# Memory's keys and values ahead of the first value chunk, and row sums taken from transposed quarters, in a two-layer encoder

## The chip, the cores and the metric

The kernel runs on one core of a Trainium2 chip. Its engines work side by side, each on its own queue in program order: TensorE (PE, with its weight loads shown as PEld), VectorE (DVE), ScalarE (ACT), GpSimd (POOL) and SyncE (SP, which only issues DMAs here). The metric is the device time of one launch in microseconds (us), the median of several runs. Only TensorE's products and transposes write PSUM, the accumulator memory of eight banks; DVE and ACT read it.

## What is computed

A trunk of two layers over 512 tokens of width 1024, with 256 memory tokens. Cut to what matters here:

```python
for i in range(2):
    h = rmsnorm(x, norm_g[i]);  mem_h = rmsnorm(mem, mem_norm_g[i])
    proj = h @ (w_in_a if i == 0 else w_in_b)      # heads, memory queries, gate
    o_mix = mixer_dilated(...) if i == 0 else mixer_axial_gqa(...)
    kv = (mem_h @ w_mem_kv[i])                      # memory's keys and values
    k, v = rmsnorm(kv[keys], kn_g), kv[values]
    o_mem = softmax(rmsnorm(q_mem) @ k.T) @ v
    y = concat(o_mix, o_mem) * silu(gate)
    x = x + y @ w_out[i]
```

All is float32.

## The kernel before

**Products in three passes.** Every float32 operand is split into a rounded part (float32r, "hi") and a remainder ("lo"). `mm3` (line 162) multiplies hi by hi, hi by lo and lo by hi. For a weight piece, 128 x 1024, `W.hi` casts it on ACT (line 285) and `W.lo` takes the remainder on DVE (line 295). For activations `split` (line 155) does the same after a transpose.

**Seven products instead of eight.** The large projections (`s_chunk`, line 352) use a Strassen-like scheme: the activation matrix is cut into four quarters 11, 12, 21, 22 and the weights likewise; seven products need the row sums S1 = 21 - 22, S2 = S1 - 11, S4 = 12 + S2, S3 = 11 - 21 of the activations, and T1 to T4 of the weights. The order of the products is 12, 11, S1, S2, S4, S3, 22. A *group* is the PE work between two calls of `W.advance`: 12 products of 512 columns, or 24 of 256. The sums of the weights are made by DVE (T1, and T2 of the very first chunk) or by DMAs that add into the tile, issued on POOL (T1 of later chunks, T2, T3, T4; lines 247 to 269). The narrower projections (memory's keys and values and half of the output projection) go through `chunk` (line 331) with plain products; one chunk of memory has four groups, each of two weight pieces and 12 products.

**Slots.** PE's groups set the order of everything else. After each group, `Driver.tick` counts one slot and steps the generators that are due: `yield n` means n slots later. `drv.free`, ahead of `W.advance`, steps those that were given to `release`; `drv.spawn` gives one to the tick, behind `W.advance`. `late` and `soon` put an instruction at the end of this tick and at the start of the next. Since each engine's queue keeps program order, what is emitted in a slot stands ahead of all that later slots emit, also if it has to wait.

**The weights.** The class `Weights` walks a plan, `PLAN`, one entry a chunk: `W2` (seven products, 512 wide), `W1` (256 wide), `T2` (a chunk of memory), `O1` (output). Pieces are loaded from DRAM by SP (line 233) while fewer than `KEEP` are live; four rounded pieces are in flight (`RING`), and a piece is cast two groups after it is loaded (`LEAD`). `NM4` = 23 tiles of 128 x 1024 are shared by weights, x, memory, gains and activations; a load waits until one is free.

**The opening.** SP loads one row of gains, then the four x tiles mixed with the first eight weight pieces (lines 839 to 852). PE spreads the gain row over 128 partitions with one-row products (`row_bank`, line 557) and does two further one-row products, `busy(512)`. The first x tile is normalized (`norm_1`: squares on ACT and DVE, the power on POOL; `norm_2`: DVE), its quarter 12 transposed (`put_h`, `turn4`) and the first product starts. The second tile's transposes stand between the first and the second half of the first group (`second`, line 905). `prep` (line 857) makes the rest: tiles 2 and 3, the row sums, their transposes, one kind a slot. `mem_norm(0)` (line 567) loads, normalizes and transposes memory while the first chunk (V of the first attention group, `ev_v0`) runs. Then come `mem_kv(0)`: two chunks of memory, keys (`ev_k`: head norms, transposes) and values (`ev_v`), and the memory queries (`s_chunk(256, H, ev_qm)`), line 959.

**The start of layer 2.** The second half of the output projection (`out_rest`, line 694) runs over four blocks of 128 tokens. For each, `ev_o` (line 1189) stores x1, normalizes it, and after `EO` slots makes the operands of layer 2: blocks 0 and 1 give the quarters 12 and 11 (transposed, split), blocks 2 and 3 give the sums in natural layout on DVE (`sum_h`, `sums_h`), and after block 3 each of S1, S2, S4, S3 and 22 is transposed for both blocks and split (`rest_h`). Meanwhile PE is in `mem_kv(1)` and then in the first projection of layer 2, the memory queries. `setup_b` (line 1221) makes the rotary tables on DVE, one operation a slot, from slot `SET_B` on.

Of the kernel before, what the change touches and what calls it, by code (L numbers as in the profile page):

```python
# [24 lines left out]
XW, BOTH = (1, 2, 0, 5), False  # L25
BULK, ACTIVE, MEM_AT, SET_AT, WARM, MEM_B, PREP_Y, ACC_AT, PREP_B, HALF, SET_B = 2, 2, 5, 15, 1, 12, 1, 4, 1, {"a": 3, "b": 3, "o": 0}, 3
MEM_STEP = 1, 1
MEM_D = 4
PD, W_EARLY = 1, True
EO = 1, 2, 2, 2, 1  # L30
# [5 lines left out]
PLAN = ["W2"] + ["T2"] * 2 + ["W1", "W2s"] + ["W2" if c.isdigit() else "W1" for c in A_ORDER[1:]] + ["W2"] + ["O1"] * 2 + ["T2b"] * 2 + ["W1b"] * 7 + ["W2b"] + ["O1"] * 2  # L36
T1_DMA = 17
KEEP = {"T2": 6, "T2b": 4, "O1": 4, "W1": 9, "W2": 10, "W2s": 9, "W1b": 7, "W2b": 9}
# [86 lines left out]
def trunk_kernel(ctx: ExitStack, tc: tile.TileContext, x, mem, wall, norm_g, mem_norm_g, gcol,  # L125
# [50 lines left out]

    class Weights:
        def __init__(self):
            self.items, self.last, self.need, self.allocs, self.sums = [], [], [], [], []
            self.users = {}  # L180
            d = g = 0
            for c, kind in enumerate(PLAN):
                base = len(self.items)
                if kind in GROUPS:
                    units, nb = GROUPS[kind]
                    for u in range(units):
                        for x in (2 * u, 2 * u + 1):
                            self.items.append((c, "P", x))
                            self.last.append(g + (u + 1) * nb - 1)
                            self.allocs.append(((c, "P", x), d, kind))  # L190
                            self.users[c, "P", x] = 1
                            d += 1
                        self.need += [base + 2 * u + 2] * nb
                    g += units * nb
                else:
                    n = 1 if kind in ("W1", "W1b") else 2
                    at = {k: d + i * n for i, k in enumerate(("21", "11", "12", "22"))}
                    d += 4 * n
# [11 lines left out]
            assert d == wall.shape[0], (d, wall.shape)  # L210
# [65 lines left out]
        def hi(self, force=False):  # L276
            i = self.n_hi
            if i >= len(self.items) or not self.ripe(self.at, self.items[i], force, 1 if self.items[i][1] == "T1" and self.items[i][0] < T1_DMA or self.items[i][:2] == (0, "T2") else None):
# [52 lines left out]
    def chunk(units, nb, group, evac):  # L331

        ps = [None] * nb
        for u in range(units):
# [132 lines left out]
    def turn4(src, hi, lo, mid=None):  # L467

        p = at("xT")
        for k in range(4):  # L470
            T.transpose(p[:, k * 128:(k + 1) * 128], src[:, k * 128:(k + 1) * 128], ident)  # L471
        if mid:
            mid()
        split(hi, lo, p.rearrange("p (k t) -> p k t", k=4))
# [10 lines left out]
    def proj_t(act, sels, evac):  # L485
# [5 lines left out]
        chunk(2, len(sels), group, evac)  # L491
# [32 lines left out]

    def head_sq(p, n=4):
# [31 lines left out]
    def row_bank(name, times=1):  # L557

        r = [at("row") for _ in range(2)]
# [33 lines left out]
    def mem_kv(layer, M):  # L593
# [3 lines left out]
        def ev_k(b, p):  # L597
            r = head_sq(p)
            yield 2
            xn = head_mul(p, r)  # L600
            yield 2
            q = transpose4(xn)
            cs = slice(b * 128, (b + 1) * 128)
            yield from put_norm(q, gk_m[layer], kt_[0][:, :, cs], kt_[1][:, :, cs])

        def ev_v(b, p):

            A.activation(vt_[0][:, b], p, AF.Copy, scale=0.5)
            yield 1
            V.scalar_tensor_tensor(vt_[1][:, b], p, 0.5, vt_[0][:, b].bitcast(F32), ALU.mult, ALU.subtract)  # L610

        proj_t(M, NAT[:2], ev_k)
# [225 lines left out]
    rows = {}  # L838
    nc.scalar.dma_start(ident, ident_d)
    row0 = m4(name="row0")[0:1, :]  # L840
    nc.sync.dma_start(row0, norm_g[0:1, :])
    rows["x0"] = halves(row0)
    for c, n in enumerate(XW):
        nc.sync.dma_start(xt[c], xv[c])
        W.dma(n)
# [3 lines left out]
    nc.sync.dma_start(mask, mask_d)  # L849
    nc.sync.dma_start(tabA, tab_a.rearrange("p (b c d) -> p b c d", b=2, c=4))  # L850
    nc.sync.dma_start(grA[:, 0:3], qn_a[0:1, :, 0:32].to_broadcast([128, 3, 32]))
    nc.sync.dma_start(grA[:, 3:6], kn_a[0:1, :, 0:32].to_broadcast([128, 3, 32]))
    H, H2 = {}, {}
    xb = [halves(t) for t in xt]
    nst = {}

    def prep():

        s1, sums = [], []
        for c in range(2):  # L860
            norm_2(xb[2 + c], nst[2 + c], first)
            s1.append(sum_h(xb[2 + c]))
# [6 lines left out]
    def setup():  # L869

        V.tensor_tensor(gk, gc[:, 0:3], gc[:, 3:6], ALU.mult)
# [10 lines left out]
    first = row_bank("x0", WARM)  # L882

    def busy(n):

        T.matmul(at("busy")[:, 0:n], ones, rows["x0"][0][0:1, 0:n], start=True, stop=True)

    busy(512)
    nst[0] = norm_1(xb[0], True)
    W.hi(True)  # L890
    norm_2(xb[0], nst[0], first, (1,))

    def mid():
        busy(128)
        W.lo()
        nst[1] = norm_1(xb[1], BOTH)

    put_h(H, "12", 0, xb[0][1], mid, True)
    if W_EARLY:
        W.hi(True)  # L900
    norm_2(xb[1], nst[1], first, (1,))
    norm_2(xb[0], nst[0], first, (0,))
    norm_2(xb[1], nst[1], first, (0,))

    def second():

        put_h(H, "12", 1, xb[1][1])
        if not W_EARLY:
            W.hi(True)
        put_h(H, "11", 0, xb[0][0])  # L910
        nst[2] = norm_1(xb[2], BOTH)
        W.lo()
        put_h(H, "11", 1, xb[1][0])
        W.hi(True)
        nst[3] = norm_1(xb[3], BOTH)
# [271 lines left out]
    x1b, sums_b = {}, []  # L1187

    def ev_o(n, b, x1):
        if n:  # L1190
# [5 lines left out]
            x1b[b] = x1  # L1196
# [319 lines left out]
```

## Time and profile before

| | us |
|---|---|
| median of 3 runs | 972.06 (971.13 to 972.48) |
| the profiled execution, whole time | 971.6 |
| its span in the trace | 969.8 |
| PE busy | 949.5 (98%) |
| DVE busy | 793.1 (82%) |
| ACT busy | 675.4 (70%) |

A row of the time-ordered view gives the start, the length, the engine, the line, the operation, the tile written and read, the shape, a count, and in brackets how long the engine stood idle before and what ended that. A row of the chain of waits gives start, length, engine and line. Lines 163 to 165 are the three passes of a product, line 471 the transposes of activations. The trace's spans of PE overlap: one product is shown as 0.39 us long while the next starts 0.23 later. The queue of SP is shown as SPq. Names of tiles: `wl` a loaded weight piece, `wh` and `wo` its parts, `pj` the accumulators of the projections, `xT` and `qT` transposes, `act` the parts of memory (M), `h` and `hS` those of the quarters and the sums.

### The profile page before, as it was taken

The numbers are of one execution on the slowest core, as the hardware profiler recorded it, in microseconds if no ns is written. First come the engines' busy times: TensorE is split into PE (matmuls) and PEld (weight loads), VectorE is DVE, ScalarE is ACT, GpSimd is POOL, SyncE is SP. The second block draws the span as 40 slices with busy tenths as digits, with TensorE's granted clock in tenths as the row PEclk, the third lists the DMA queues.
The fourth block names the chain that finished last, engine by engine and source line by source line (L and its number), as shares of the span: only waits on it lengthen the run. The fifth ranks groups of instructions, "written<-read, shape, count | busy, mean of one in ns | idle before, by whom it ended". The sixth has DMA issues, their size and how long they took to land. (4 is left out here: it accounts for less than half of the span.)

```text
span 969.8 us, 16665 instructions
## 1 busy us (share of the span) xinstructions
PE 949.5 (98%) x5728; PEld 835.8 (86%) x5728; DVE 793.1 (82%) x1413; ACT 675.4 (70%) x1687; POOL 332.7 (34%) x480
## 2 busy tenths in 40 slices
PE   8899999999999999999999999999999999999998
PEld 5689988888888888888899996787999999998776
DVE  6997776888888888888898999769888997779863
ACT  6555689686868686868685667545778887878760
POOL 1122423556454545454736011323233231011011
PEclk9999999999999999999999999999999999999999
DMA  8979846968787868685959889959986696786644
GB/s 331 326 267 336 220 102 170 293 131 259 150 256 154 256 153 261 154 260 131 279 134 233 259 203 272 299 191 351 240 178 148 178 241 166 218 213 163 183 140 130
DMA packets 88982, 209.27 MB, mean 216 GB/s; under 512 B 25281, under 2 KB 36033, under 8 KB 88898
## 3 DMA queue, kind: packets, MB, share of 16 engines
q1 hardware_dynamic: 70034, 146.28, 43.5%
q0 software_dynamic: 17568, 59.78, 32.5%
q10 hardware_dynamic: 1296, 2.16, 0.6%
q8 instruction: 45, 0.74, 0.3%
q14 instruction: 39, 0.32, 0.1%
HBM read 157.79 MB, written 12.65 MB: 176 GB/s over the span
## 5 line engine op out<-in xcount | busy, mean ns | idle before, releaser
L295 DVE TENSOR_TENSOR wo<-wl,wh 128x1024 fp32r<-128x1024 f32 x255 | 314.6, 1237 | 12.3 <-ACT wh L285 11.5
L285 ACT CAST wh<-wl 128x1024 fp32r<-128x1024 f32 x255 | 269.7, 1059 | 75.7 <-PE pj L165 39.8
L163 PE MATMUL pj<-wh,hS 128*128 128x512 f32 (+1 forms) x448 | 164.3, 367 | 0.0
L164 PE MATMUL pj<-wo,hS 128*128 128x512 f32 (+1 forms) x448 | 158.1, 353 | 2.6 <-DVE wo L295 2.6
L165 PE MATMUL pj<-wh,hS 128*128 128x512 f32 (+1 forms) x448 | 158.2, 353 | 0.0
L163 PE MATMUL pj<-wh,h 128*128 128x512 f32 (+1 forms) x336 | 123.4, 367 | 0.0
L164 PE MATMUL pj<-wo,h 128*128 128x512 f32 (+1 forms) x336 | 118.8, 354 | 2.3 <-DVE wo L295 2.3
L165 PE MATMUL pj<-wh,h 128*128 128x512 f32 (+1 forms) x336 | 118.9, 354 | 0.0
L420 POOL TENSOR_TENSOR rstd<-mse,half 128x4 f32<-128x4 f32 (+2 forms) x98 | 100.1, 1021 | 8.2
L164 PEld LDWEIGHTS pj<-wo,hS 128*128 128x128 f32 x448 | 85.0, 190 | 13.4 <-DVE wo L295 3.5
L165 PEld LDWEIGHTS pj<-wh,hS 128*128 128x128 f32 x448 | 84.7, 189 | 12.4 <-DVE hS L160 0.3
L163 PEld LDWEIGHTS pj<-wh,hS 128*128 128x128 f32 x448 | 84.8, 189 | 9.7
L419 POOL TENSOR_SCALAR mse<-hss 128x4 f32<-128x4 f32 (+1 forms) x86 | 44.3, 515 | 129.9 <-ACT junk L529 126.1
L360 ACT COPY sn<-pj 128x512 f32<-128x512 f32 x132 | 73.6, 591 | 14.3 <-PE pj L165 10.7
L529 ACT ACTIVATE junk<-sn 128x128 f32<-128x128 f32 x264 | 79.0, 308 | 0.2 <-DVE sn L371 0.2
L987 POOL TENSOR_TENSOR ta<-sn,tabs 128x128 f32<-128x128 f32 (+1 forms) x64 | 37.2, 584 | 119.7 <-DVE sn L534 91.6
L164 PEld LDWEIGHTS pj<-wo,h 128*128 128x128 f32 x336 | 64.0, 190 | 10.0 <-DVE wo L295 2.8
L165 PEld LDWEIGHTS pj<-wh,h 128*128 128x128 f32 x336 | 63.7, 190 | 9.3 <-DVE h L160 0.2
L163 PEld LDWEIGHTS pj<-wh,h 128*128 128x128 f32 x336 | 63.9, 190 | 7.3 <-ACT h L157 0.2
L377 DVE TENSOR_TENSOR sn<-pj,sn 128x512 f32<-128x512 f32 x99 | 67.5, 683 | 3.0 <-PE pj L165 2.6
L269 POOL DMA_DIRECT2D wl<-wl x33 | 29.3, 886 | 112.4 <-DVE wo L295 70.7
L163 PE MATMUL pj<-hS,wh 128*128 128x256 f32 x192 | 55.9, 291 | 0.0
(229 smaller groups left out, 2457.1 us busy)
## 6 DMA issues: line engine op xcount, KB each, us to landing
wl<-in_wall_dram SPq DMA_DIRECT2D x222, 512.0 KB, 6.9
wl<-wl POOLq DMA_DIRECT2D x64, 512.0 KB, 5.8
wl<-in_wall_dram POOLq DMA_DIRECT2D x42, 512.0 KB, 8.5
acc<-sn POOLq DMA_DIRECT2D x16, 256.0 KB, 5.0
od<-o SPq DMA_DIRECT2D x12, 256.0 KB, 5.2
og<-od SPq DMA_DIRECT2D x12, 256.0 KB, 6.8
odb<-o SPq DMA_DIRECT2D x12, 256.0 KB, 2.7
og<-odb SPq DMA_DIRECT2D x12, 256.0 KB, 3.9
```

What stands on the lines that cost most here:

```text
L163: T.matmul(o, lh, rh, start=start, stop=False, skip_group_check=True)
L164: T.matmul(o, lh, rl, start=False, stop=False, skip_group_check=True)
L165: T.matmul(o, ll, rh, start=False, stop=stop, skip_group_check=True)
L269: G.dma_start(self.tile[key], self.tile[c, "T2", x], accum_op=ALU.add)
L285: A.copy(wh, self.tile[self.items[i]])
L295: V.tensor_tensor(wo, self.tile[key], wh.bitcast(F32), ALU.subtract)
L360: A.copy(t, b)
L377: V.tensor_tensor(t, b, t, ALU.subtract if q == "12" else ALU.add)
L419: G.tensor_scalar(e, ss, EPS, None, ALU.add)
L420: G.tensor_tensor(r, e, half[:, 0:n], ALU.pow)
L529: A.activation(jk, p[:, j * 128:(j + 1) * 128], AF.Square, scale=QS, accum_out=ss[:, j:j + 1])
L987: G.tensor_tensor(ta[:, 0:n], xn[:, 0:n, 0:32], ropeA[:, 0, b, s0:s0 + n], ALU.mult)
```

## The change

**Opening.** Memory's two tiles and its gain row are loaded first, each followed by a weight piece, and x after that. A second gain row, x's, is spread by PE into two more accumulators (`gain`) and copied to SBUF by ACT later; `busy(512)` is dropped. PE begins with the two memory chunks; `ahead`, called before each group of the first one, transposes the second tile's first half ahead of the second group and both second halves ahead of the third. `prep` now does all four x tiles from slot 2 on, one a slot, and the sums from slot 7. The first V chunk follows; `mem_norm(0)` goes. `SEQ` gives the order of the chunks, with the weights in DRAM left where they are. T2 of the first V chunk is a DMA like the others. The loads of mask and rotary tables move into `setup` (slot 15).

**Evacuation of `chunk`.** Accumulators are read from `drv.free`, ahead of the weight work of the next group, instead of from the tick behind it; `ev_k` and `ev_v` are cut accordingly.

**Layer 2.** Each block's quarters are transposed once; the sums are formed from the transposed quarters (one of them in PSUM), already in the layout of the operands, and split without a transpose. Blocks 2 and 3 are done separately, casts on ACT at once, remainders on DVE at the end of the tick. `EO` has six values; `SET_B` goes from 3 to 1.

```diff
-XW, BOTH = (1, 2, 0, 5), False
-PD, W_EARLY = 1, True
-EO = 1, 2, 2, 2, 1
+PD = 2
+EO = 2, 2, 1, 2, 2, 1
+SEQ = [1, 2, 0] + list(range(3, len(PLAN)))
...
-                    if c:
-                        G.dma_start(self.tile[key], self.tile[c, "T1", x], accum_op=ALU.add)
-                    else:
-                        V.tensor_tensor(self.tile[key], self.tile[key], self.tile[c, "T1", x], ALU.add)
+                    G.dma_start(self.tile[key], self.tile[c, "T1", x], accum_op=ALU.add)
...
+                if pre:
+                    pre(u, b)
                 group(w, u, b, ps[b])
                 drv.free()
+                if u == units - 1:
+                    drv.release(evac(b, ps[b]), 2)
                 W.advance()
-                if u == units - 1:
-                    drv.spawn(evac(b, ps[b]), 2)
                 drv.tick()
...
+    def first_t(H, top, c):
+        ps = [(k, turn4(top[j], *slot(H, k, c))) for k, j in (("12", 1), ("11", 0))]
+        for k, p in ps:
+            A.copy(whole(k, c), p)
+    def diffs_t(H, low, c):
+        f22 = whole("22", c)
+        A.copy(f22, turn4(low[1], None, None))
+        p = turn4(low[0], None, None)
+        yield 1
+        s1, s3 = whole("S1", c), whole("S3", c)
+        V.tensor_tensor(s1, p, f22, ALU.subtract)
+        V.tensor_tensor(s3, full["11"][:, :, c * 128:(c + 1) * 128], p, ALU.subtract)
+        split(*slot(H, "S1", c), s1)
+    def rest_t(H, c, ds):
+        def put(k, f):
+            hi, lo = slot(H, k, c)
+            A.copy(hi, f)
+            drv.late(lambda: V.tensor_tensor(lo, f, hi.bitcast(F32), ALU.subtract))
+        cs = slice(c * 128, (c + 1) * 128)
+        s1, s2_, s4, s3, f22 = [full[k][:, :, cs] for k in ("S1", "11", "12", "S3", "22")]
+        V.tensor_tensor(s2_, s1, s2_, ALU.subtract)
+        V.tensor_tensor(s4, s4, s2_, ALU.add)
+        put("S2", s2_)
+        yield ds[0]
+        put("S4", s4)
+        yield ds[1]
+        put("S3", s3)
+        yield ds[2]
+        put("22", f22)
+        yield 1
...
         def ev_k(b, p):
             r = head_sq(p)
-            yield 2
-            xn = head_mul(p, r)
-            yield 2
-            q = transpose4(xn)
+            def rest():
+                xn = head_mul(p, r)
+                yield 2
+                q = transpose4(xn)
...
+            drv.release(rest(), 2)
+            yield 1
...
+    for b in range(2):
+        nc.sync.dma_start(mt[b], mem[b * 128:(b + 1) * 128])
+        W.dma(1)
+    W.dma(2)
...
+    for c in range(4):
+        nc.sync.dma_start(xt[c], xv[c])
+        if c % 2:
+            W.dma(2)
...
     def prep():
+        s1, sums, n = [], [], {}
+        for c in range(5):
+            if c < 4:
+                n[c] = norm_1(xb[c])
+            if c:
+                norm_2(xb[c - 1], n[c - 1], rows["x"])
+                if c > 2:
+                    s1.append(sum_h(xb[c - 1]))
+            if 1 < c < 4:
+                put_h(H, "12", c - 2, xb[c - 2][1])
+                put_h(H, "11", c - 2, xb[c - 2][0])
             yield 1
         for c in range(2):
             sums_h(H, xb[c], xb[2 + c], c, s1[c], sums)
-            yield 1
+            yield 2 - c
         yield from rest_h(H, sums)
...
-    busy(512)
-    nst[0] = norm_1(xb[0], True)
+    mb, M = [halves(t) for t in mt], Act(NM)
+    nst = [norm_1(mb[0], True)]
...
+    def ahead(u, b):
+        if (u, b) == (0, 1):
+            for j in range(2):
+                A.copy(rows["x"][j], gain[j])
+            norm_3(mb[1], M, 128, 0)
+            for c in range(2):
+                norm_2(mb[c], nst[c], first, (1,))
+        if (u, b) == (1, 0):
+            for c in range(2):
+                norm_3(mb[c], M, 128 * c, 1)
...
-    drv.spawn(mem_norm(0), MEM_AT)
-    s_chunk(512, H, ev_v0, pre=second)
-    km, vm = mem_kv(0, Ms[0])
+    km, vm = mem_kv(0, M, ahead)
+    s_chunk(512, H, ev_v0)
...
             if b < 2:
-                put_h(H2, "12", b, x1[1])
-                put_h(H2, "11", b, x1[0])
+                first_t(H2, x1, b)
             else:
-                s1 = sum_h(x1)
+                yield from diffs_t(H2, x1, b - 2)
                 yield EO[2]
-                sums_h(H2, x1b[b - 2], x1, b - 2, s1, sums_b)
-            if b == 3:
-                yield EO[3]
-                yield from rest_h(H2, sums_b, EO[4])
+                yield from rest_t(H2, b - 2, EO[3:])
```

More of the change, by code (lines that the diff above doesn't have):

```diff
@@ L180, in __init__ @@
             self.users = {}
-            d = g = 0
-            for c, kind in enumerate(PLAN):
+            g = 0
+            for c in SEQ:
+                kind, d = PLAN[c], sum(pieces(k) for k in PLAN[:c])
                 base = len(self.items)
@@ L209, in __init__ @@
                             g += 1
-            assert d == wall.shape[0], (d, wall.shape)
+            assert sum(pieces(k) for k in PLAN) == wall.shape[0]
             self.g = -1
@@ L329, in trunk_kernel, with chunk @@
     W = Weights()
-    def chunk(units, nb, group, evac):
+    def chunk(units, nb, group, evac, pre=None):
         ps = [None] * nb
@@ L555, in row_load, with row_bank @@
         rows[name] = halves(t)
-    def row_bank(name, times=1):
-        r = [at("row") for _ in range(2)]
+    def row_bank(name, times=1, bank=at):
+        r = [bank("row") for _ in range(2)]
         for j in (1, 0):
@@ L838, in trunk_kernel @@
     rows = {}
+    mt = [m4(name="m") for _ in range(2)]
     nc.scalar.dma_start(ident, ident_d)
     row0 = m4(name="row0")[0:1, :]
[L841 to L845, printed above, removed]
+    nc.sync.dma_start(row0, mem_norm_g[0:1, :])
+    rows["m0"] = halves(row0)
+    row1 = m4(name="row1")[0:1, :]
+    nc.sync.dma_start(row1, norm_g[0:1, :])
+    rows["x0"] = halves(row1)
+    for b in range(2):
+        nc.sync.dma_start(mt[b], mem[b * 128:(b + 1) * 128])
+        W.dma(1)
+    W.dma(2)
     tabA = s2(name="tabA")[:, 0:256].rearrange("p (b c d) -> p b c d", b=2, c=4)
@@ L880, in setup @@
             yield 1
-    first = row_bank("x0", WARM)
+    first = row_bank("m0", WARM)
+    gain = row_bank("x0", 1, pj)
+    rows["x"] = halves(m4(name="row"))
     def busy(n):
-        T.matmul(at("busy")[:, 0:n], ones, rows["x0"][0][0:1, 0:n], start=True, stop=True)
-    busy(512)
-    nst[0] = norm_1(xb[0], True)
+        T.matmul(at("busy")[:, 0:n], ones, rows["m0"][0][0:1, 0:n], start=True, stop=True)
+    mb, M = [halves(t) for t in mt], Act(NM)
+    nst = [norm_1(mb[0], True)]
     W.hi(True)
-    norm_2(xb[0], nst[0], first, (1,))
+    norm_2(mb[0], nst[0], first, (0,))
     def mid():
@@ L895, in mid @@
         W.lo()
[L896 to L915, printed above, removed]
+        nst.append(norm_1(mb[1]))
+    turn4(mb[0][0], M.block(0, 0, slice(0, 128)), M.block(1, 0, slice(0, 128)), mid)
+    W.hi(True)
+    norm_2(mb[1], nst[1], first, (0,))
+    W.lo()
+    def ahead(u, b):
[8 more added lines that the diff above has]
+                norm_3(mb[c], M, 128 * c, 1)
     drv.spawn(prep(), PD)
```

56 lines of the change are left out of this document (33 added, 23 removed).

## The prediction

> **What bounds the kernel now.** I read the page's busy shares first, then the stretches of 20 us, then TensorE's waits, then the time-ordered rows of the opening and of the start of layer 2.
>
> ```profile
> span 969.8 us, 16665 instructions
> PE 949.5 (98%) x5728; PEld 835.8 (86%) x5728; DVE 793.1 (82%) x1413; ACT 675.4 (70%) x1687; POOL 332.7 (34%) x480
> ```
>
> TensorE (PE) is without work for 20.3 us of 969.8. An edit can help where PE waits, or by taking work from PE itself.
>
> ```profile
> 0.00:20.00 20.00, 16.77 (x51) 10.79 (x52) 11.19 (x18) 12.54 (x26) 4.54 (x16) 1.00 0.90 340
> 20.00:40.00 20.00, 15.42 (x76) 11.83 (x75) 19.97 (x26) 9.58 (x14) 3.69 (x4) 1.00 0.99 296
> ...
> 660.00:680.00 20.00, 18.82 (x109) 15.69 (x108) 19.96 (x29) 10.78 (x29) 7.58 (x8) 1.00 1.04 336
> ```
>
> Columns after the length: PE, weight loads, DVE, ACT, POOL, granted clock, DMA share, GB/s. Both places that the change touches are the ones where PE loses time, and in both DVE is full: 19.97 of 20 us at 20-40, 19.96 at 660-680. The waits name it:
>
> ```profile
> PE pj L164 <- DVE wo L295: 6.7, 8, 2.0
> ```
>
> PE waits there for a weight piece's remainder (line 295), which stands in DVE's queue behind the preparation of activations.
>
> **Prices.** From the time-ordered rows:
>
> ```profile
> 64.20 0.39 PE L163 MATMUL pj<-wh,act 128*128 128x512 f32 x1
> ```
>
> ```profile
> 644.88 0.23 PE pj L165
> 645.10 0.23 PE pj L163
> ...
> 656.88 0.89 PE xT L471 x8
> ```
>
> ```profile
> 46.46 1.29 DVE L160 TENSOR_TENSOR h<-xT,h 128x512 fp32r<-128x512 f32 x2 [1.19 <-ACT h L157]
> 47.67 2.44 DVE L295 TENSOR_TENSOR wo<-wl,wh 128x1024 fp32r<-128x1024 f32 x2
> ...
> 54.41 1.41 DVE L465 SCALAR_TENSOR_TENSOR m<-m,rstd,row 128x512 f32<-128x512 f32 x2
> ```
>
> A 512-column product costs PE 0.228 us (96 of them run from 64.20 to 85.97 below), a transpose 0.11. Two instructions in a row overlap by some 0.08, so DVE pays 0.60 for a 512-wide two-input operation, 1.14 to 1.2 for a 1024-wide one, 0.66 for a normalization.
>
> **The opening, before.**
>
> ```profile
> 0.73 0.35 SPq L841 DMA_DIRECT2D row<-in_norm_g_dram  x1
> ...
> 1.14 0.37 SPq L844 DMA_DIRECT2D x<-in_x_dram  x1
> ...
> 2.24 3.75 PE L562 MATMUL row<-row,ones 1*128 1x512 f32 x4 [2.24 <-DMA row<-in_norm_g_dram]
> ...
> 5.78 1.91 PE L886 MATMUL busy<-row,ones 1*128 1x512 f32 x2
> ...
> 9.65 0.80 PE L163 MATMUL pj<-wh,h 128*128 128x512 f32 x1
> ...
> 10.68 0.63 PE L165 MATMUL pj<-wh,h 128*128 128x512 f32 x1
> ...
> 11.10 0.63 PE L163 MATMUL pj<-wh,h 128*128 128x512 f32 x1
> ...
> 12.38 1.64 PE L471 MATMUL xT<-ident,x 128*128 128x128 f32 x8
> ...
> 14.84 0.66 PE L471 MATMUL xT<-ident,x 128*128 128x128 f32 x4 [0.81 <-DVE h L160]
> ```
>
> ```profile
> 7.06 0.75 DVE L465 SCALAR_TENSOR_TENSOR x<-x,rstd,row 128x512 f32<-128x512 f32 x1 [1.36 <-POOL rstd L420]
> ...
> 7.87 1.11 PE L471 MATMUL xT<-ident,x 128*128 128x128 f32 x4 [0.17 <-DVE x L465]
> ...
> 9.02 0.58 ACT L157 CAST h<-xT 128x512 fp32r<-128x512 f32 x1
> ...
> 85.97 0.60 PE L541 MATMUL qT<-ident,xn 128*128 128x128 f32 x4
> ```
>
> The first product starts at 9.65 and the work of the first V chunk and of memory's keys and values ends at 85.97. It holds 168 + 96 products (60.2 us) and 68 transposes (7.4). So 76.3 - 67.6 = 8.7 us are lost, to waits and to the first products, which run at 0.42 until about 14.
>
> **The opening, after.** Products and transposes are the same in number, so three things decide.
>
> Start. PE gets a second gain row (four passes more at 0.85 each, by the x4 row) and loses the two busy passes: it is free at about 2.24 + 8 x 0.85 = 9.0, not 7.7. The memory tile, one row later in SP's queue (0.4 us), is normalized by 8.2 (x: 7.06 + 0.75), so now PE is late. Four transposes at 0.2, a cast of 0.6 and the hand-over put the first product at 10.7: +1.05.
>
> Slow products. Twelve in a row instead of six broken by transposes; with the same 4 us or so until full pace, 8 to 10 run 0.2 too long: 1.6 to 2.0 us.
>
> DVE. I step the queues in program order, each instruction starting when its engine is free and its inputs are there. From 10.7 to the remainder of V's first piece, DVE has 12 operations of 0.60 (M's 4 remainders, 4 of H, 2 head products, 2 differences), 11 normalizations of 0.66 and 10 of 1.14 (8 weight remainders, 2 T1 sums): 25.9 us. It stands idle 3.2 us for the second half of M and about 2.6 elsewhere, mostly because the first casts of x stand on ACT behind squares and two weight casts. The remainder is done at 42.5. PE by then has 21.9 of products, about 1.8 of slow pace, 36 transposes (3.9) and 2.5 of small waits: 1.2 for M's casts and remainders at the second group, 0.7 at the third, 0.6 for x's differences. That is 40.8. It waits 1.7. The next nine or so microseconds of DVE (three more weight remainders, two S1 remainders, three sums, four halves of memory's keys and values, then the S2 sum of the second block) end at 52.2. The transposes of that S2 block stand in PE's queue at 48.9, because the preparation emits S2 one group after S1, four groups before it is needed: 3.3 more. After that ACT and DVE have air. Waits 7.5, slow pace 1.8, sum 9.3 against 8.7 lost before; with the later start +1.65. The slow products may be ten rather than nine, so I take **+1.9 us**. Bounds: without the 1.7 and the 3.3 it is -3.1; with loads late by 3 us (below) +5.
>
> Hidden, at nothing: the T2 sums of V leave DVE (2 x 1.2) for POOL, whose copies
>
> ```profile
> wl<-wl POOLq DMA_DIRECT2D x64, 512.0 KB, 5.8
> ```
>
> land in about 6 us (median) and are read four groups of 2.7 us after the sum is due; if the cover went, PE would wait once for the difference, under 3. The 512 KB row load goes; two ACT copies replace it in an idle stretch of ACT. Table loads move behind slot 15; they are read by the first head, some 50 us later. SP queues 14 half-megabyte loads at the start instead of 12; at the 340 GB/s of the first 20 us they are in by 21.6 us, x's last tile before that, and it is squared after 30. V's T1 pieces must wait for free buffers (23 in all, 15 held by x, memory, M, its keys, values and row): about 30, read at 33.
>
> **Layer 2.** Ten groups of four transposes (S1, S2, S4, S3, 22 of two blocks) give way to four (22 and 21): 56 transposes become 32, so 24 x 0.11 = **-2.6 us** of PE's own time. DVE has 22 operations before (2 differences, 6 sums, 14 remainders) and 22 after. ACT gets 6 copies more, 0.54 each; it has 9 of 20 us free. The order is what changes:
>
> ```profile
> 657.65 1.42 DVE L465 SCALAR_TENSOR_TENSOR acc<-acc,rstd,row 128x512 f32<-128x512 f32 x2 [1.45 <-DMA x1d<-acc]
> ...
> 663.78 0.22 DVE L1222 TENSOR_SCALAR grB<-grB 128x128 f32<-128x128 f32 x1
> 664.03 0.69 DVE L1225 TENSOR_TENSOR tabs<-tbraw,grB 128x512 f32<-128x512 f32 x1
> ...
> 669.92 0.68 DVE L514 TENSOR_TENSOR xs<-xs,acc 128x512 f32<-128x512 f32 x1
> ...
> 677.00 0.68 DVE L516 TENSOR_TENSOR xs<-acc,xs 128x512 f32<-128x512 f32 x1
> ...
> 688.31 1.20 DVE L295 TENSOR_TENSOR wo<-wl,wh 128x1024 fp32r<-128x1024 f32 x1
> ```
>
> ```profile
> 39.16 1.10 ACT L360 COPY sn<-pj 128x512 f32<-128x512 f32 x2
> ...
> 671.78 1.05 ACT L285 CAST wh<-wl 128x1024 fp32r<-128x1024 f32 x1 [0.81 <-PE pj L165]
> 676.85 1.05 ACT L285 CAST wh<-wl 128x1024 fp32r<-128x1024 f32 x1 [4.02 <-DMA wl<-wl]
> ```
>
> ```profile
> 682.56 0.36 PE L163 MATMUL pj<-wh,hS 128*128 128x256 f32 x1
> ```
>
> DVE runs without a pause from 657.65 to 689.5. Before, the sums went through PE's transposes to ACT; now ACT's casts of S1 and S2 read DVE's sums directly, and DVE is behind. Stepping the queues again: DVE takes up the second block's 12 and 11 remainders at 663.3, after waiting 2 us for ACT, whose copies and head squares stand ahead of those casts. Then come a table (0.6), two normalizations (1.3), two head products (1.2), four weight remainders (4.6), the first quarter differences (1.3) and S1's remainder (0.6): the first S2 sum starts at 674.2 and ends near 675. ACT, in order, does S2's cast then, the second S1 cast after the second difference (676.2), key and value, and only at 677.8 T1's weight cast, 6 us later than the 671.78 above. On DVE T1's remainder stands behind eleven more operations, 8.2 us, and ends at 683.6. PE gets to its first product on S1 (682.56 above) some 2 us sooner by the saved transposes, at 680.6, and that group wants the remainder at once: **+3.0**. The tables, moved two slots up, put 2 to 3 DVE operations into DVE's idle time
>
> ```profile
> 640.00:660.00 20.00, 20.00 (x98) 16.75 (x97) 11.34 (x15) 11.47 (x23) 5.78 (x13) 1.00 0.81 296
> ```
>
> before 660, where it is busy 11.34 of 20 us (a part of that walk; left in place they would make the wait 1.2 longer). Evacuations ahead of weight work cost a remainder 0.6 of delay at most, covered by two groups of lead. 3.0 - 2.6 is 0.4; some of the 1.2 us that PE loses now at 660-680 goes with it, so **+0.2**. Bounds: -2.6 (the remainder is not late) and +2 (it is late again at S2).
>
> Sum: 971.6 (the profiled execution: span 969.8 and 1.8 around it) + 1.9 + 0.2 = 973.7. That execution lies 0.46 under the median of 972.06, so **974.2**.
>
> **Rivals.**
> A, faster: DVE keeps up. If it is idle for less than the 3.2 before M's second half, the S2 transposes find their sum ready and 3.3 goes, with 0.2 of the 1.7; with T1's cast in time layer 2 gives 2.2. 972.06 - 1.6 - 2.2 = 968.3. For: DVE has no more work than before, 2.4 less. Against: both stretches were already full. It decides if DVE is under 3 us behind at V's second group.
> B, they cancel: one of the two late steps comes, the other not; 1.9 - 2.2 or -1.4 + 1.5: 972.
> C, the clock. One-row products kept PE busy from 2.24 to 7.69, yet the pace was 0.42 at 10.7-11.1 (the granted clock reads 1.00 throughout). If eight passes, 6.8 us, release it before the first product, 8 to 12 products and 4 transposes gain 0.2 or 0.1 each, some 2.4: 971.8. [...]
> D, slower by more: T1's piece lands after 33 and its sum, on DVE's in-order queue, holds all preparation behind it. Each microsecond late is one lost; 3.5 gives 977.7. For: DMA's share is 0.90 and 0.99 in the first two stretches, and every buffer is taken. Against: 3 us of margin.
>
> **Numbers.** Forecast 0.35 (973 to 976), A 0.28, B 0.22, C 0.05, D 0.10. This measurement tells about 0.2%, 1.9 us, from no change. Faster is A: 0.28. Same is B, C and the forecast's lower edge (0.05): 0.32. Slower 0.40. The range reaches from A with the T1 wait also gone in full, 967, to D: 978.
>
> **What would show it.** First product at 10.5 to 11. A PE wait for a weight remainder near 41 and for S2's sum near 49, DVE busy over 19 of 20 us at 30-50; the 85.97 work, less its 8 key transposes, ends near 88. In layer 2, 32 activation transposes, and one wait of 2 to 4 us on T1's remainder in the first memory-query groups. I am wrong if 30-50 shows PE at 20 of 20 (then A), or a wait on a weight DMA shows on DVE before 35 (then D).

## The result, and the profile after

The changed kernel takes 976.57 us (median of 6; 975.70 to 978.75), beside 971.60 for the kernel before on the same chip: 1.0053 times as long, 95% interval 1.0041 to 1.0065, some 5 us slower. Of the runs reported below, one execution (of covered_row_loaded) took 1225.66 us at a mean granted clock of 0.717; it is in no ratio. The changed kernel's profiled execution is the slowest of the six, 978.75 us with a span of 976.8, so its end is not compared; its stages are.

In the changed kernel lines 164 to 166 are the three passes of a product, 475 the transposes of activations, 297 the remainder of a weight piece. Its page, span and engines:

```profile
span 976.8 us, 16652 instructions
PE 952.7 (98%) x5706; PEld 837.4 (86%) x5706; DVE 790.2 (81%) x1411; ACT 680.0 (70%) x1695; POOL 342.6 (35%) x482
```

PE is busy 3.2 us longer with 22 instructions fewer. So the loss is not in waits alone: some instructions took longer. The same stretches of 20 us as before (PE, weight loads, DVE, ACT, POOL, granted clock, DMA share, GB/s):

```profile
0.00:20.00 20.00, 16.77 (x40) 9.56 (x41) 7.99 (x13) 10.43 (x19) 2.19 (x10) 1.00 0.89 349
20.00:40.00 20.00, 19.40 (x100) 15.67 (x99) 17.24 (x23) 16.31 (x45) 12.73 (x17) 1.00 0.90 350
40.00:60.00 20.00, 15.34 (x65) 12.14 (x64) 17.15 (x23) 8.20 (x12) 4.42 (x5) 0.83 0.94 221
...
680.00:700.00 20.00, 17.14 (x131) 16.94 (x130) 18.07 (x25) 15.49 (x30) 5.36 (x6) 0.91 1.03 317
```

In the first 20 us PE is busy as long as before (16.77), from 20 to 40 longer (19.40, before 15.42). But 40 to 60, where PE was full before with 106 instructions, has 65, and the granted clock reads 0.83; 680 to 700 reads 0.91. Before, both read 1.00. PE's waits, by what ended them:

```profile
PE pj L165 <- DVE wo L297: 5.1, 4, 2.9
PE xT L475 <- DVE xs L521: 3.2, 1, 3.2
```

Both waits that were forecast are there. In order of time, PE's rows of the opening:

```profile
2.56 7.16 PE L622 MATMUL row<-row,ones 1*128 1x512 f32 x8 [2.56 <-DMA row<-in_mem_norm_g_dram]
...
11.44 0.80 PE L164 MATMUL pj<-wh,act 128*128 128x512 f32 x1
...
44.09 0.50 PE L165 MATMUL pj<-wo,h 128*128 128x512 f32 x1 [1.50 <-DVE wo L297]
...
53.70 1.09 PE L475 MATMUL xT<-ident,xs 128*128 128x128 f32 x4 [3.17 <-DVE xs L521]
54.44 0.78 PE L164 MATMUL pj<-wh,h 128*128 128x512 f32 x1
55.02 0.63 PE L165 MATMUL pj<-wo,h 128*128 128x512 f32 x1
...
59.65 1.03 PE L475 MATMUL xT<-ident,xs 128*128 128x128 f32 x8
60.44 0.48 PE L164 MATMUL pj<-wh,h 128*128 128x512 f32 x1
60.75 0.39 PE L165 MATMUL pj<-wo,h 128*128 128x512 f32 x1
```

Look at the lengths behind the wait of 3.17 us (it begins at 50.53): 0.63 at 55.02, and 0.39 again at 60.75. One product starts every 0.43 us there, half the pace of 0.23, until 59.65. Twelve products take 5.21 instead of 2.74 us, the four transposes 0.74 instead of 0.35: 2.9 us that no wait shows. What the wait was for, DVE's rows of the changed kernel:

```profile
49.35 2.35 DVE L297 TENSOR_TENSOR wo<-wl,wh 128x1024 fp32r<-128x1024 f32 x2
51.62 0.74 DVE L650 SCALAR_TENSOR_TENSOR kmT<-qT,gc,kmT 128x512 fp32r<-128x512 f32 x1
52.28 0.68 DVE L161 TENSOR_TENSOR hS<-xT,hS 128x512 fp32r<-128x512 f32 x1
52.88 0.68 DVE L521 TENSOR_TENSOR xs<-xs,x 128x512 f32<-128x512 f32 x1
```

The S2 sum (line 521) stands behind remainders that nobody needs yet. A mark to compare by are the transposes of `pmt` that wait 0.6 us for ACT near 156 us, past all that the change touches in layer 1. They start at 156.00 before and at 161.43 after: the opening costs 5.4 us in this execution. The mark has a scatter of its own: layer2_alone, whose layer 1 is that of the kernel before, has it at 157.3, since there the first weight piece landed later and the first product started at 10.93 instead of 9.65. In layer 2 the wait for T1's remainder is 2.86 us, and it too is followed by slow products (one in 0.21 instead of 0.12 us), though not at once: the first four run at full pace.

```profile
687.00 0.38 PE L165 MATMUL pj<-wo,hS 128*128 128x256 f32 x1 [2.86 <-DVE wo L297]
687.23 0.28 PE L166 MATMUL pj<-wh,hS 128*128 128x256 f32 x1
...
687.76 0.42 PE L164 MATMUL pj<-wh,hS 128*128 128x256 f32 x1
687.97 0.42 PE L165 MATMUL pj<-wo,hS 128*128 128x256 f32 x1
...
691.11 0.28 PE L165 MATMUL pj<-wo,hS 128*128 128x256 f32 x1
691.23 0.28 PE L166 MATMUL pj<-wh,hS 128*128 128x256 f32 x1
```

From memory's first product of layer 2 to the first product on its keys it is 76.21 us (651.85 to 728.06), beside 76.29 before (647.66 to 723.95): up to there layer 2 costs nothing.

### The profile page after: what moved, and what is told of

Read it like the earlier page. It is cut to its first block, busy times and chain, and to the rows that moved or that the text cites. A ratio compares the mean times of both kernels' runs of the same rounds, so it can differ in the third digit from the quotient of the medians.

```text
span 976.8 us, 16652 instructions
## 1 busy us (share of the span) xinstructions
PE 952.7 (98%) x5706; PEld 837.4 (86%) x5706; DVE 790.2 (81%) x1411; ACT 680.0 (70%) x1695; POOL 342.6 (35%) x482
## 4 chain that ended last, share of the span: by engine, by line
PE 80%; DVE 8%; DMA 7%; ACT 3%; issue 1%; SPq 0%; DVEq 0%; ACTq 0%; POOLq 0%
PE pj L166 21%; PE pj L164 21%; PE pj L165 21%; DMA wl<-in_wall_dram 3%; DVE wo L297 3%; PE qT L601 2%; PE sa L1122 1%; PE oo L1224 1%; PE pt L1203 1%; PE sa L1118 1%; DMA odb<-o 1%; PE ptb L1421 1%; PE ob L165 1%; DMA acc<-sn 1%; ACT wh L287 1%
## 5 line engine op out<-in xcount | busy, mean ns | idle before, releaser
L424 POOL TENSOR_TENSOR rstd<-mse,half 128x4 f32<-128x4 f32 (+2 forms) x98 | 102.9, 1050 | 8.2
```

The source lines that it names most:

```text
L424: G.tensor_tensor(r, e, half[:, 0:n], ALU.pow)
```

## The experiments

"Ratio" is to the kernel before on the same chip, with its 95% interval. "Mark" is the start of those `pmt` transposes in the profile (156.00 before, 161.43 after).

| run | ratio | interval | mark, us |
|---|---|---|---|
| opening_alone | 1.0047 | 1.0030 to 1.0064 | 161.0 |
| layer2_alone | 1.0006 | 0.9993 to 1.0019 | 157.3 |
| s2_two_later | 0.9989 | 0.9978 to 1.0001 | 155.9 |
| fill_products | 1.0022 | 1.0010 to 1.0034 | 158.1 |
| fill_rows | 1.0055 | 1.0034 to 1.0076 | 160.9 |
| both_later | 1.0020 | 1.0008 to 1.0032 | 155.6 |
| s4_sum_later | 1.0012 | 1.0002 to 1.0022 | 155.7 |
| later_prep_sooner | 1.0054 | 1.0036 to 1.0071 | 157.0 |
| later_row_loaded | 1.0013 | 0.9997 to 1.0030 | 154.1 |
| s4_later_row_loaded | 0.9979 | 0.9967 to 0.9991 | 154.5 |
| x3_later | 1.0004 | 0.9991 to 1.0018 | 153.7 |
| covered_row_loaded | 0.9969 | 0.9954 to 0.9983 | 155.9 |

**Which half costs the time.** opening_alone is the changed kernel with `ev_o` and its delays as before; layer2_alone is the kernel before with the new `ev_o`, `first_t`, `diffs_t`, `rest_t`.

> The changed kernel with layer 2 built as before (row sums through ten groups of transposes, its old delays, tables at the third slot). Theory: the opening carries the whole loss. PE waits about 3 us for the S2 sum near 50 us, the products after it run at 0.43 instead of 0.23 us, and the 256-wide memory-query products start 5 to 6 us later than before; 4.5 to 6 us over the kernel before, 976 to 977.6 where that one takes 971.6. Rival: the opening loses only the wait (some 3 us) and the rest is lost in layer 2 and behind it: 974 to 975.

> The kernel before with only layer 2's row sums from transposed quarters (its delays, casts and remainders apart, tables at the first slot). Theory: 24 transposes fewer (2.6 us) and the small waits at 660 to 680 (1.2) against one wait for the remainder of T1 (2.9) and a slow stretch of some 3.5 us after it (1.7): within 1 us of the kernel before, 971 to 972.6. Rival: the loss between 728 and 923 us in the changed kernel comes from layer 2: 2 to 4 us over the kernel before, 973.6 to 975.6.

1.0047 and 1.0006 make up the whole 1.0053. The loss is the opening's; its wait is 3.12 us again. Layer 2 alone can't be told from no change, as the theory had it, but not by the wait that it named. In its profile PE waits for a bank that ACT copies out late, probably because this kernel keeps the old order of evacuations (no run tested that), and no slow stretch follows. That holds for this execution, whose mean granted clock is 1.000; ten of the twelve runs read 0.994 to 0.998.

```profile
682.22 0.39 PE L163 MATMUL pj<-wh,hS 128*128 128x256 f32 x1 [2.61 <-ACT sn L360]
682.45 0.28 PE L164 MATMUL pj<-wo,hS 128*128 128x256 f32 x1
682.56 0.28 PE L165 MATMUL pj<-wh,hS 128*128 128x256 f32 x1
```

**Is it the place of S2's transposes.** In `prep`:

```diff
             sums_h(H, xb[c], xb[2 + c], c, s1[c], sums)
-            yield 2 - c
+            yield 2 + c
```

> The changed kernel with one number changed: layer 1's S2 transposes are emitted two groups later (they are still read two groups after that). Theory: the 3.2 us wait at 50.5 comes only from the place of these transposes in PE's queue; the wait goes, and with it the stretch at half pace behind it (2.4 us): 4 to 5.5 us under the changed kernel, 971 to 972.5, and the granted clock at 40 to 60 us reads 1.00. Rival: DVE is the bound there whatever the order; PE then waits at the next weight remainder instead: less than 1.5 us gained, 975 to 976.5.

0.9989, that is 0.0064 or 6.2 us under the changed kernel's ratio: a little more than expected. The same stretch, of this kernel:

```profile
40.00:60.00 20.00, 18.19 (x89) 14.56 (x88) 19.78 (x26) 10.23 (x14) 4.42 (x5) 1.00 0.98 220
```

Clock 1.00, and of the wait 0.28 us is left, at a weight remainder. DVE now works 19.78 of 20 us, so it has no more to give there, but it needed no more: one number puts the opening level with the one before.

**Is it the wait that slows the products, and what counts as work.** Neither run saves any waiting; both put useless PE work into the wait, ahead of the second block's S2 transposes.

```diff
+    def cover():
+        p = at("busy").rearrange("p (a t) -> p a t", a=2)
+        for _ in range(13):
+            T.matmul(p, part["12"][:, 0, 0, 0:128], part["12"][:, 0, 0:2, :], start=True, stop=True)
...
             for c in range(2):
+                if k == "S2" and c:
+                    cover()
                 put_h(H, k, c, sums[c][i])
```

fill_rows has three `T.matmul(p, ones, rows["m0"][0][0:1, :], ...)` in `cover` instead; the trace shows them as six records.

> The changed kernel with 13 products on old operands (some 3 us of PE, results unused) set into the wait ahead of the second block's S2 transposes. They save no waiting. Theory: the wait itself lets the clock drop, so with PE kept busy the 12 products after it take 0.23 us each, not 0.43, and the granted clock at 40 to 60 us reads 1.00: 2 to 2.5 us under the changed kernel, near 974.3. Rival: the slow pace has another cause than the wait; the products after it stay at 0.43 and the time stays at 976.6 or rises by some tenths.

> The changed kernel with three passes on one row (128 columns out of one partition, 512 wide, some 0.9 us each) set into the wait of 3.2 us instead of 13 products on all rows. If the clock goes by whether PE has instructions, they hold it: products behind the wait at 0.23 us, 2 to 2.5 us under the changed kernel, as with 13 products. If it goes by how much of the array works, one row in 128 is as good as idle: the products behind it run at 0.43 us for 3.4 to 6 us and the time is that of the changed kernel, 1.004 to 1.0065 of the kernel before.

With 13 products in the wait:

```profile
49.76 3.24 PE L505 MATMUL busy<-h 128*128 128x512 f32 x13
53.17 0.63 PE L475 MATMUL xT<-ident,xs 128*128 128x128 f32 x4 [0.16 <-DVE xs L526]
53.55 0.48 PE L164 MATMUL pj<-wh,h 128*128 128x512 f32 x1
53.87 0.40 PE L165 MATMUL pj<-wo,h 128*128 128x512 f32 x1
```

With passes on one row:

```profile
49.88 3.50 PE L505 MATMUL busy<-row,ones 1*128 1x512 f32 x6
53.31 1.11 PE L475 MATMUL xT<-ident,xs 128*128 128x128 f32 x4
54.08 0.78 PE L164 MATMUL pj<-wh,h 128*128 128x512 f32 x1
54.65 0.63 PE L165 MATMUL pj<-wo,h 128*128 128x512 f32 x1
```

The transposes start at about the same time (53.17 and 53.31). Behind the products the pace is 0.23 and the mark comes 3.3 us sooner than after the change (0.3 of it from an earlier start); behind the passes it is 0.43, as behind the idle wait, and the ratio is that of the changed kernel. The granted clock at 40 to 60 us reads 1.00 with the products and 0.83 with the passes, as after the change. So here the idle wait slowed the products, and 3.50 us of passes on one row in its place did not prevent that.

**Layer 2's wait.** Two ways to let T1's remainder pass S2's work. Both are made on s2_two_later. both_later:

```diff
-EO = 2, 2, 1, 2, 2, 1
+EO = 2, 2, 2, 1, 2, 1
```

s4_sum_later keeps `EO` and has in `rest_t`:

```diff
-        V.tensor_tensor(s4, s4, s2_, ALU.add)
         put("S2", s2_)
-        yield ds[0]
+        yield ds[0] - c
+        V.tensor_tensor(s4, s4, s2_, ALU.add)
+        yield 1
         put("S4", s4)
-        yield ds[1]
+        yield 1 + c
```

> The changed kernel with S2 emitted later in both layers: layer 1 as in the run with one number changed; in layer 2 the sums and casts of S2 one group later (third delay 1 to 2), S4 where it was (fourth delay 2 to 1). Theory: T1's weight cast then no longer stands behind the first S2 cast on ACT, and its remainder no longer behind three DVE operations of the second block: it comes some 2.3 us sooner, the wait of 2.9 at the first S1 group shrinks under 1 and, being short, leaves the clock at full speed: 3 to 4 us under the run with layer 1 alone, 0.993 to 0.996 of the kernel before. Rival: DVE works there without a pause, so the wait only moves to S2's remainder one group later: under 1.5 us gained, 0.997 to 0.999.

> The run with layer 1's S2 two groups later, and in layer 2 S2 left where the change put it, but S4's two sums taken out from behind S2's and put behind T1's remainder on DVE; S4's casts of the first block one group later, beside the second's. Theory: DVE, not the order, bounds that place, so only work taken from ahead of T1's remainder counts: two sums of 0.6 make the wait 1.65 instead of 2.85 us, and a wait that short leaves the clock at full pace (1.7 us more); some of it is lost again at S2's group, whose bank DVE frees late: 1.5 to 2.5 us under the run with layer 1 alone, 0.996 to 0.998 of the kernel before. Rival: the wait comes back in full at S2's group, as with S2 later: no gain, 0.999 to 1.002.

Both lose 2 to 3 us to s2_two_later. The first wait shrinks (1.41 and 2.10 us), and a second one comes at S2's group: 3.41 and 2.05. In both_later, PE then DVE:

```profile
679.80 0.38 PE L165 MATMUL pj<-wo,hS 128*128 128x256 f32 x1 [1.41 <-DVE wo L297]
...
686.21 0.35 PE L164 MATMUL pj<-wh,hS 128*128 128x256 f32 x1 [3.41 <-ACT hS L569]
```

```profile
682.78 1.28 DVE L570 TENSOR_TENSOR hS<-f,hS 128x512 fp32r<-128x512 f32 x2
684.77 0.69 DVE L570 TENSOR_TENSOR hS<-f,hS 128x512 fp32r<-128x512 f32 x1 [0.71 <-ACT hS L569]
685.38 0.68 DVE L381 TENSOR_TENSOR sn<-pj,sn 128x512 f32<-128x512 f32 x1
```

The wait is booked on an ACT cast, but S2 accumulates into the bank that line 381 reads, and that read ends at 686.06, just before PE goes on; it stands behind three remainders of activations. That reading is from the rows; no run removed it. The runs fit the rival's mechanism: DVE is short of time there, and the order only chooses who waits. both_later came out worse even than its rival's 0.997 to 0.999, because its two waits add up to 4.82 us where s2_two_later has one of 2.85; either profile has one slow stretch there.

**Gains elsewhere in the opening.** later_prep_sooner is made on both_later:

```diff
-PD = 2
+PD = 1
...
-            yield 2 + c
+            yield 2 + 2 * c
```

x3_later is made on s4_later_row_loaded, in `prep`:

```diff
                 put_h(H, "11", c - 2, xb[c - 2][0])
-            yield 1
+            yield 2 if c == 3 else 1
...
-            yield 2 + c
+            yield 2
```

The loaded row is made on both_later (later_row_loaded) and on s4_sum_later (s4_later_row_loaded):

```diff
-    row1 = m4(name="row1")[0:1, :]
-    nc.sync.dma_start(row1, norm_g[0:1, :])
-    rows["x0"] = halves(row1)
...
         nc.sync.dma_start(xt[c], xv[c])
+        if c == 2:
+            row_load("x", norm_g[0:1, :])
...
-    gain = row_bank("x0", 1, pj)
-    rows["x"] = halves(m4(name="row"))
...
-            for j in range(2):
-                A.copy(rows["x"][j], gain[j])
```

> The kernel with both S2 later, and the preparation of x started one group sooner (its delay 2 to 1; S2 and what follows stay where they were). Theory: DVE is idle for over 5 us at 10 to 30 us and short of time at 35 to 45; moving norms and remainders forward takes the 1.5 us wait for V's first weight remainder near 42.6 away: 1 to 1.5 us under the kernel with both later. Rival: the squares and casts of x then stand on ACT ahead of memory's casts, for which PE waits already (0.7 at 16.6): what is won is lost there, within 0.5 us.

> The kernel with both S2 later, and x's gain row loaded into all partitions by a transfer (512 KB, behind x's third tile) instead of four one-row passes and two copies. Theory: the four passes delay the start; the first product moves from 11.4 to about 10 us, and as passes on one row do not bring the array to full pace anyway, all of it is kept: 1 to 1.5 us under the kernel with both later. Rival: the passes do count for the clock; the products then run at half pace for longer and the two cancel within 0.5 us; or x's last tile and weights come later by the 512 KB and PE waits for them once.

> The kernel with S4's sums later, and x's gain row loaded by a transfer instead of one-row passes. Theory: the first product at 10.0 instead of 11.4 us and all of layer 1 sooner by the same 1.45, as the profile of the same edit showed with both S2 later: 0.9945 to 0.9965 of the kernel before, faster than both kernels. Rival: the later stages take it back (1.9 instead of 0.8 us of waits near 912): within 0.5 us of the run without it.

> The kernel with S4's sums later and the row loaded, and x's last tile normalized and subtracted one group later (S1 of the first block goes one group later too, S2 stays). Theory: two normalizations and a difference (1.9 us of DVE) then stand behind V's weight remainders near 41 instead of ahead, and the 1.5 us wait there goes; some 0.5 comes back near 50, where DVE is busy 19.7 of 20 us: 0.5 to 1.2 us under the run before it. Rival: DVE is the bound over the whole of 35 to 55 us, the wait moves to 50 in full or, over 2.6 us long, costs the clock: no gain or a loss.

Sooner preparation is a miss: 0.0034 slower than both_later. A new wait of 1.10 us at 22.28, for a remainder of memory's activations that x's work now delays on DVE, and the wait near 43 is 1.79 us, no shorter. Its mark is 1.45 us later; besides, the slow stretch of layer 2 is twice as long in its profile (6.8 us, in both_later 3.4). x's last tile later only moves that wait: from 41 to 46, and from 1.53 to 2.40 us. It is a miss too: 0.0025 slower than s4_later_row_loaded, though its profile has the mark 0.7 us sooner; where the runs lose it was not found.

The loaded row moves the first product as forecast, here of later_row_loaded:

```profile
7.53 1.11 PE L475 MATMUL xT<-ident,m 128*128 128x128 f32 x4 [1.50 <-DVE m L469]
8.57 0.79 PE L965 MATMUL busy<-row,ones 1*128 1x128 f32 x2
9.32 0.79 PE L164 MATMUL pj<-wh,act 128*128 128x512 f32 x1
```

9.32 instead of 11.13 us, but then 10 products run slow instead of 8, so the mark moves by 1.45 (1.2 in s4_later_row_loaded). The 10 is not a price of the early start: x3_later starts at 9.24 and has 8 slow ones and part of a ninth (the last section has the other starts). The ratios fall by 0.0007 in the one pair and 0.0033 in the other; the gain that was expected lies between them, but 0.9979 misses the 0.9945 to 0.9965 that were forecast for s4_later_row_loaded, since s4_sum_later, on which it is made, had missed its own 0.996 to 0.998. Both profiles also lose some of the gain near 914 us, where waits of 1.92 and 2.35 us are followed by a slow stretch that the kernels without the loaded row do not have.

**All that helped, with layer 2's wait filled.** covered_row_loaded has s2_two_later's number, the loaded row, `rest_t` as the change has it, and in `s_chunk`, for layer 2's memory queries alone:

```diff
+            if a == cover:
+                p = at("busy").rearrange("p (a t) -> p a t", a=2)
+                for _ in range(10):
+                    T.matmul(p, act["12"][:, 0, 0, 0:128], act["12"][:, 0, 0:2, :], start=True, stop=True)
             if fresh:
...
-    s_chunk(256, H2, ev_qmb)
+    s_chunk(256, H2, ev_qmb, cover="S1")
```

> The kernel with layer 1's S2 two groups later and x's gain row loaded; layer 2 as the change has it, with S4's sums back in their place, and ten products on old operands (2.3 us of PE, results unused) ahead of the first S1 group there. They save no waiting for T1's remainder, they only keep PE at work. Theory: first product at 10.0 us; the wait of 2.85 shrinks to about 0.5, the remainder comes no sooner, and the 14 or more products behind it take 0.12 instead of 0.21 us each: 1.45 and 1.7 us under the run with layer 1's S2 later, 0.995 to 0.9965 of the kernel before, the fastest of all. Rival: the slow stretch comes anyway, from a later wait or because ten products are too few, or the fill delays the transposes and evacuations queued behind it: 0.997 to 0.9985, no better than with S4's sums later.

```profile
679.91 2.46 PE L392 MATMUL busy<-h 128*128 128x512 f32 x10
682.21 0.28 PE L164 MATMUL pj<-wh,hS 128*128 128x256 f32 x1
683.06 0.39 PE L165 MATMUL pj<-wo,hS 128*128 128x256 f32 x1 [0.58 <-DVE wo L297]
...
683.40 0.28 PE L164 MATMUL pj<-wh,hS 128*128 128x256 f32 x1
```

No slow product follows, and at 0.9969 it is faster than both kernels, its interval clear of 1. It falls short of the sum of its parts (0.9989 less 1.45 and 1.7 us, 0.9957): a wait of 0.67 us comes at S2's group, and in its profile the row's gain is lost again: the first weight piece landed at 7.35 instead of 5.95 us, PE waited 1.27 us for a cast that stood behind it on ACT, and 12 products ran slow (mark 155.9). Its ratio lies between what was expected and what its rival expected, and the interval covers most of both.

## Why the prediction held, and where its sum fell short

The direction and the range were right; the time, 974.2, was 2.4 us short of 976.57, and the change more so: +2.1 us forecast, +5.0 measured. 976.57 lies above the 973 to 976 that the forecast gave itself 0.35. What holds it in the range is the upper edge of D, and D's cause did not come: that is luck. Taken by its steps:

**Start.** Forecast 10.7 us, measured 11.44 (11.13 to 11.37 in the profiles of the seven other kernels with this start). The gain row landed 0.3 us later than in the profile before, and a pass takes 0.895, not 0.85. The start costs 1.8, not 1.05.

**Waits.** V's first remainder near 41 (1.7): 1.50 at 42.59. S2's sum near 49 (3.3): 3.17 at 50.5. The small ones (2.5): 1.3. In all 5.9 us behind the first product; before it was 5.4. DVE worked 19.35 of 20 us from 30 to 50, as forecast. s2_two_later shows that the S2 wait was what the prediction said, a matter of the transposes' place in PE's queue: emitted two groups later, they leave 0.28 us of it.

**The step that failed** is "Waits 7.5, slow pace 1.8, sum 9.3". It counts the slow pace at the start alone and takes a wait to cost its own length. A wait of 3.17 us cost 3.17 and 2.9 more; fill_products shows it by keeping the wait and losing the slow pace. The opening's 1.9 us should have been 1.8 + 0.5 + 2.9 = 5.2, beside the 5.4 measured. Counted in the prediction's own way, the stretch from 11.44 to 92.25 us (with the 8 key transposes) loses 12.3 us instead of 9.3: waits 5.9, the slow start 1.8, the second slow stretch 2.9, and 1.7 of small losses between transposes and products, for which the sum has no term although the 8.7 of before holds 1.2 of them. The waits came out 1.6 us under the forecast, which hid more than half of the missing 2.9; that too is luck. The trace of the kernel before did not show this cost: its longest wait for a remainder is 2.0 us, and its granted clock reads 1.00.

**Layer 2.** Forecast +0.2, measured -0.1 in the profile and +0.6 (-0.7 to +1.8) in layer2_alone. There are 32 transposes of activations, and one wait of 2.86 us (3.0 forecast) on T1's remainder. The slow products behind it (15 of them, 1.4 us) were missing here too. What balances them, from the same rows of both profiles: the 24 transposes give back 2.5 us as forecast, the small waits of 660 to 680 are gone in full (1.15 us, where the sum took 0.2), and 0.6 more is saved between products and transposes. So the step was right in its wait and right in its total because its omissions cancel.

**Rivals.** A fell: DVE did not keep up. C fell: after 7.2 us of one-row passes the first eight products ran at 0.43, and in fill_rows those behind 3.50 us of such passes did too. D fell: no weight DMA held DVE at 33. B fell: both late steps came.

## What to carry to other kernels

Price a wait of TensorE together with the products behind it. Here the wait of 3.17 us cost 2.9 us beyond its length, in 6.8 us at half clock, and the one of 2.86 us cost 1.4, in 3.4 us; those of 2.40 (x3_later) and 2.61 us (layer2_alone) had no slow product behind them. So look at the granted clock of the stretch, not at busy time alone. Transposes that depend on a full vector engine go as late into TensorE's queue as their readers allow; that one number was worth the whole loss (6.2 us, s2_two_later). Where the vector engine was the bound, reordering only moved a wait in the runs here, but products that do nothing, put into it, saved the pace: 0.23 us a product in fill_products where the changed kernel has 0.43, and 0.12 in covered_row_loaded where s2_two_later has 0.21.

## What the hardware showed that was not expected

**Which waits were followed by half clock.** The length of the wait alone does not decide it. Single waits of 2.85 (s2_two_later), 2.86 and 3.17 (both after the change) and 3.12 us (opening_alone) were followed by a slow stretch, and so were 1.92 and 2.35 (later_row_loaded and s4_later_row_loaded, near 914); 2.04, 2.40 (both x3_later) and 2.61 (layer2_alone) were not. In s4_sum_later products run at 0.12 us behind a wait of 2.10 us and at 0.21 behind one of 2.05, 5 us later. After the change the granted clock is half from 52.73 to 59.55 and from 687.61 to 691.02, and full between them. Rows of 3.41 or 3.42 us around such waits, of the changed kernel, layer2_alone and later_row_loaded (columns as above):

```profile
49.31:52.73 3.42, 1.23 (x8) 0.81 (x6) 3.42 (x5) 0.59 (x1) 2.69 (x3) 1.00 1.08 280
52.73:56.14 3.41, 2.44 (x8) 2.18 (x9) 3.32 (x7) 1.31 (x3) 0.00 (x0) 0.50 1.07 213
56.14:59.55 3.41, 3.41 (x9) 2.59 (x9) 1.13 (x1) 1.19 (x2) 0.00 (x0) 0.50 1.06 211
59.55:62.97 3.42, 3.42 (x20) 2.90 (x19) 2.07 (x3) 2.02 (x3) 0.00 (x0) 1.00 0.26 52
```

```profile
677.11:680.52 3.41, 2.50 (x21) 2.30 (x20) 2.03 (x3) 3.05 (x6) 1.79 (x2) 1.00 1.05 280
680.52:683.94 3.42, 1.72 (x14) 1.72 (x15) 3.42 (x6) 3.42 (x7) 0.00 (x0) 1.00 1.05 352
```

```profile
911.55:914.96 3.41, 1.49 (x7) 0.90 (x6) 3.41 (x6) 2.66 (x6) 0.54 (x1) 1.00 0.83 238
914.96:918.37 3.41, 3.41 (x11) 2.56 (x10) 3.41 (x7) 3.03 (x6) 0.33 (x1) 0.50 0.43 78
```

In the row ahead of a drop PE worked 1.23 us (to 52.73) and 1.49 us (to 914.96), and 0.60 us in the 3.42 us ahead of 687.61. The wait of 2.61 us lies in two rows, with 2.50 and 1.72 us of work, and the clock reads 1.00 in both. What decides between the waits was not shown.

The slow stretches differ in length too. The wait of 3.17 us after the change has 6.8 us and twelve products at half pace behind it; the same wait in opening_alone (3.12 us) has six and part of a seventh, from 55.14 to 58.12. The start differs likewise: fill_products, both_later and s2_two_later all start their first product at 11.13, and the first one at full pace starts at 14.59, 15.02 and 15.84. The number of slow products there is 6 to 12 in the 14 profiles.

**Passes on one row did not bring or keep the pace.** Eight passes on one partition at the start (7.16 us after the change) and six records in fill_rows (3.50 us) kept PE busy without a gap, and the products behind both ran at 0.43 us. At 40 to 60 us PE is busy for 18.50 of 20 us in fill_rows and for 18.31 in fill_products; the granted clock reads 0.83 in the one and 1.00 in the other.

**The spread of one kernel's runs may have the same cause.** Of later_row_loaded's twelve runs one took 968.06 us, at a mean granted clock of 1.000; the other eleven, at 0.994 to 0.998, took 972.22 to 977.71. A stretch of 3.41 us at half clock in 972 us, as the one from 687.61 after the change, makes a mean of 0.998, and three make 0.995. Of these runs one alone was traced, so the link is not shown; at up to 1.7 us for 3.41 it covers only a part of the spread.
